# Time mixing in 11 slots with the inverse folded in, modulation products held behind the tile in front, and the normed activation made four tiles at a time

## The chip, the core and the metric

The kernel runs on one NeuronCore of a Trainium2 chip. Five engines work beside each other, each through its own list of instructions in order: TensorE (PE, with PEld for its weight loads), VectorE (DVE), ScalarE (ACT), GpSimd (POOL) and SyncE (SP), which issues nearly all transfers. An instruction that waits holds up everything behind it on its engine. The metric is the device time of one execution in microseconds (us), and less is better.

## The reference

Two layers over 256 tokens of width 2048, all in float32, one sample. Layer 0 mixes over time (RWKV-7), layer 1 is attention in chunks of 64, each followed by an MLP of width 8192 with a squared ReLU. Ahead of each part the input is normed (RMS) and modulated by a shift and a scale which come, like the gates, from the vector `c`:

```python
for layer in range(DEPTH):
    mod = c @ w_ada[layer] + b_ada[layer]
    sh1, sc1, gt1, sh2, sc2, gt2 = jnp.split(mod, 6, axis=-1)
    if layer == N_A_LAYERS:
        sh_kv, sc_kv = jnp.split(c @ w_ada_kv + b_ada_kv, 2, axis=-1)
        h_kv = modulate(rms_norm(x, g_kv), sh_kv, sc_kv)      # keys, values
    h = modulate(rms_norm(x, g_mix[layer]), sh1, sc1)
    ...                                                       # time mixing or attention
    x = x + gt1[:, None, :] * y
    h = modulate(rms_norm(x, g_mlp[layer]), sh2, sc2)
    x = x + gt2[:, None, :] * sq_relu_mlp(h, w_up[layer], w_down[layer])
return rms_norm(x, g_final)
```

Time mixing has 32 heads of 64. For each a state S runs over the tokens:

```python
sa = jnp.einsum('bhvk,bhk->bhv', S, -kk_t)
S = (S * w_t[:, :, None, :] + sa[..., None] * (kk_t * a_t)[:, :, None, :]
     + v_t[..., None] * k_t[:, :, None, :])
y = jnp.einsum('bhvk,bhk->bhv', S, r_t)
```

followed by a norm per head, a term with r, k and v, a gate, and the output projection.

## The kernel before

Activations lie with the model's 2048 channels on 16 tiles of 128 partitions, 256 tokens wide. Nearly all of the time goes to products with weights of 2048 rows. Float32 precision is made from two reduced-precision (fp32r) parts: ACT casts a weight half of 128x1024 to `wH` (L366), DVE subtracts it from the `raw` weights to give `wL` (L369), and the activation is a pair `aHL` in the same way. For each of 16 blocks of rows (kt) PE runs one 512-wide matmul with `wH` over both parts of the activation (L400) and one 256-wide matmul with `wL` (L401); a tile of 128 output channels is 16 such pairs. Transfers of weights land in a ring `raw` of six 512 KB slots, `wH` and `wL` have three slots each.

The modulation is a product of the vector `c` with 16 x 2048 columns per part; DVE makes it as running sums (`acc`, L430), one transfer of 512 KB for each, and PE adds up 128 rows at the end of 16 (L442, 128x1 matmuls). These products run between other work: a call of `ada` takes one further, and calls stand in the loops of time mixing, MLP0 and attention. In MLP0 their ring is `rawm` with six slots, in attention `rawt` with two.

Time mixing handles a pair of heads (128 channels) at a time, 16 pairs, in a pipeline four deep: while the wide matmuls project k and r for pair j, the generators `early`, `invert` and `late` run for the three pairs ahead of it. `invert` builds the inverse of a unit triangular 64x64 matrix per chunk of 64 tokens, in doubling levels of 32x32 tiles; `late` goes over the four chunks in turn and carries the state `zs`. Each round of the pipeline is cut into 16 slots; a slot runs each generator by its share of steps (up to a `yield`), then a share of the wide matmuls, and the order on PE is tied to this by `issue_after`. Small matmuls are of 64x64 or 32x32 tiles of PE's array, several side by side.

At three places, called seams here (the first tiles of MLP0, of attention and of MLP1), the next product would need x normed over all channels, which is known only when all of x is there. The first eight tiles (`SCALED`) run on x times gain without the norm, with two more columns for the shift (258-wide, L389 to L391), and are multiplied with `rstd` afterwards. `rstd` needs the sum over all channels (`m`, L494), a logarithm and an exponential on ACT (L498, L499) and some steps on DVE (L496, L501 to L504). Meanwhile `normed` makes the normed activation for the tiles from the ninth on: per channel tile a product with `rstd` on POOL (L519), two activations on ACT (L521), one subtraction on DVE (L522).

The tile framework orders each engine's instructions by its own list scheduling within the given dependencies, so an edit can also move instructions that it doesn't name.

## Time and profile before

| | us |
|---|---|
| runs shown | 2738.26 (median), 2733.71, 2740.51 |
| profiled execution | 2732.68, its span 2730.7 |
| PE busy | 2645.1 (97%) |
| DVE busy | 2041.8 (75%) |
| ACT busy | 1363.3 (50%) |
| POOL busy | 361.0 (13%) |

The span is a chain of stages: the low-rank products and the value projection to about 231 us, time mixing to 744, output projection to 806, MLP0 to 1538 (its first eight tiles to 859), attention's keys, values and scores to 1897, its output projection to 1988, MLP1 to 2717. The page gives totals of the whole span; the windows give them by stage. In the timeline a row has start, duration, engine, line, operation, output and inputs, shape and count, and in brackets the idle time ahead of it with what ended it. Matmuls overlap, so the cost of one on PE is read from start to start, not from its duration.

### The profile page before, as it was taken

How to read it: one execution, taken by the hardware profiler on the slowest of the kernel's cores; microseconds unless marked ns; L12 is line 12 of the kernel's file. 1: busy time of each engine (PE TensorE's matmuls, PEld its weight loads, DVE VectorE, ACT ScalarE, POOL GpSimd, SP SyncE). 2: the span in 40 equal slices, each digit the busy share in tenths (PEclk: the TensorE clock that was granted, in tenths of full speed). 3: DMA queues.
4: the chain of work that ended last, by engine and by line, in shares of the span. 5: the costliest groups of instructions: out<-in, count | busy, mean ns of one | idle time of the engine just before them, and what ended most of it. 6: DMA issues, size and time to landing. Idle time of an engine off the chain costs nothing.

```text
span 2730.7 us, 59448 instructions
## 1 busy us (share of the span) xinstructions
PE 2645.1 (97%) x24298; PEld 2250.2 (82%) x24298; DVE 2041.8 (75%) x2986; ACT 1363.3 (50%) x2457; POOL 361.0 (13%) x480
## 2 busy tenths in 40 slices
PE   6999999999999999999999899999999999999997
PEld 5787777777889888888888888877888888888886
DVE  5568777878799687788888788899996655566554
ACT  3346555555457543345544474465465533455443
POOL 0003434443212000000000130000120000000011
PEclk9999999999999999999999999999999999999999
DMA  9866546555688688888888778988875555555553
GB/s 349 299 243 197 172 157 191 191 170 167 214 301 286 224 284 302 316 315 315 308 307 309 249 241 310 329 307 279 283 267 194 185 190 188 187 190 186 190 188 124
DMA packets 192817, 662.70 MB, mean 243 GB/s; under 512 B 21409, under 2 KB 36129, under 8 KB 192545
## 3 DMA queue, kind: packets, MB, share of 16 engines
q1 hardware_dynamic: 190480, 656.36, 70.3%
q8 instruction: 191, 3.13, 0.5%
q10 hardware_dynamic: 2064, 2.54, 0.3%
q14 instruction: 82, 0.66, 0.1%
HBM read 656.72 MB, written 2.10 MB: 241 GB/s over the span
## 4 chain that ended last, share of the span: by engine, by line
PE 77%; DVE 7%; DMA 5%; issue 2%; ACT 2%; POOL 1%; DVEq 0%; SPq 0%; POOLq 0%; ACTq 0%
PE pj L400 41%; PE pj L401 20%; DMA rawt<-w_ada 3%; DVE wL L369 2%; PE iv L106 2%; DVE acc L430 2%; PE gr L100 1%; PE pj L391 1%; PE pj L390 1%; PE pj L389 1%; PE o L389 1%; DMA rawm<-w_ada 1%; ACT wH L366 1%; PE ms L100 1%; PE chn L279 1%
## 5 line engine op out<-in xcount | busy, mean ns | idle before, releaser
L400 PE MATMUL pj<-aHL,wH 128*128 128x512 f32 x4352 | 1574.7, 402 | 4.0 <-DVE ks L962 1.2
L369 DVE TENSOR_TENSOR wL<-raw,wH 128x1024 fp32r<-128x1024 f32 x772 | 951.5, 1234 | 421.7 <-ACT wH L366 419.1
L366 ACT CAST wH<-raw 128x1024 fp32r<-128x1024 f32 x772 | 805.9, 1046 | 878.3 <-PE pj L400 767.5
L401 PE MATMUL pj<-aHL,wL 128*128 128x256 f32 x4352 | 1226.6, 282 | 4.8 <-DVE wL L369 4.4
L400 PEld LDWEIGHTS pj<-aHL,wH 128*128 128x128 f32 x4352 | 821.2, 189 | 203.0 <-issue 11.5
L401 PEld LDWEIGHTS pj<-aHL,wL 128*128 128x128 f32 x4352 | 822.5, 189 | 12.0 <-DVE wL L369 9.5
L400 PE MATMUL pj<-hHL,wH 128*128 128x512 f32 x1024 | 359.0, 394 | 0.0
L401 PE MATMUL pj<-hHL,wL 128*128 128x256 f32 x1024 | 284.2, 278 | 0.0
L489 POOL TENSOR_TENSOR ss<-ss,sq 128x256 f32<-128x256 f32 x56 | 55.2, 986 | 1477.3 <-ACT sq L488 1477.1
L400 PEld LDWEIGHTS pj<-hHL,wH 128*128 128x128 f32 x1024 | 192.0, 188 | 44.5
L430 DVE SCALAR_TENSOR_TENSOR acc<-rawm,ct,acc 128x1024 f32<-128x1024 f32 x165 | 215.3, 1305 | 10.5 <-DMA rawm<-w_ada_kv 6.3
L401 PEld LDWEIGHTS pj<-hHL,wL 128*128 128x128 f32 x1024 | 192.3, 188 | 0.0
L430 DVE SCALAR_TENSOR_TENSOR acc<-rawt,ct,acc 128x1024 f32<-128x1024 f32 x100 | 129.7, 1297 | 21.4 <-DMA rawt<-w_ada 21.1
L430 DVE SCALAR_TENSOR_TENSOR acc<-raw,ct,acc 128x1024 f32<-128x1024 f32 x95 | 127.4, 1341 | 0.8 <-DMA raw<-w_ada 0.6
L389 PE MATMUL pj<-aHL,wH 128*128 128x258 f32 x384 | 112.4, 293 | 9.4 <-DVE ks L976 7.1
L391 PE MATMUL pj<-aHL,wL 128*128 128x258 f32 x384 | 111.4, 290 | 5.6 <-DVE wL L369 5.5
L390 PE MATMUL pj<-aHL,wH 128*128 128x258 f32 x384 | 111.7, 291 | 2.4 <-DVE aHL L513 2.4
L926 DVE SCALAR_TENSOR_TENSOR x<-pj,mod,x 128x256 f32<-128x256 f32 x128 | 61.7, 482 | 38.9 <-PE pj L401 37.2
L519 POOL TENSOR_TENSOR sq<-x,rstd 128x256 f32<-128x256 f32 x64 | 67.7, 1070 | 125.1 <-DVE aHL L522 70.7
L389 PEld LDWEIGHTS pj<-aHL,wH 128*128 128x128 f32 x384 | 75.1, 195 | 10.7 <-issue 7.3
L391 PEld LDWEIGHTS pj<-aHL,wL 128*128 128x128 f32 x384 | 75.9, 198 | 7.0 <-DVE wL L369 6.5
L390 PEld LDWEIGHTS pj<-aHL,wH 128*128 128x128 f32 x384 | 75.3, 196 | 3.0 <-DVE aHL L513 2.8
(255 smaller groups left out, 3026.6 us busy)
## 6 DMA issues: line engine op xcount, KB each, us to landing
raw<-w_up SPq DMA_DIRECT2D x256, 512.0 KB, 4.3
raw<-w_down SPq DMA_DIRECT2D x256, 512.0 KB, 3.9
rawm<-w_ada SPq DMA_DIRECT2D x111, 512.0 KB, 6.0
rawt<-w_ada SPq DMA_DIRECT2D x107, 512.0 KB, 4.7
raw<-w_ada SPq DMA_DIRECT2D x102, 512.0 KB, 4.2
rawa<-w_ada SPq DMA_DIRECT2D x64, 512.0 KB, 6.5
rawm<-w_ada_kv SPq DMA_DIRECT2D x64, 512.0 KB, 6.5
raw<-w_k SPq DMA_DIRECT2D x32, 512.0 KB, 4.0
```

Of the source, the lines that this page charges most:

```text
L100: self.b.nc.tensor.matmul(o(c)[K], lhsT(c)[K], rhs(c)[K], start=True, stop=True)
L366: nc.scalar.copy(Hf, raw)
L369: eng.tensor_tensor(out=Lf, in0=raw, in1=Hf, op=ALU.subtract)
L389: nc.tensor.matmul(ps, H[:, i, :], a(kt)[:, 0, :], start=(first and kt == 0), stop=False)
L390: nc.tensor.matmul(ps, H[:, i, :], a(kt)[:, 1, :], start=False, stop=False)
L391: ins = nc.tensor.matmul(ps, L[:, i, :], a(kt)[:, 0, :], start=False, stop=(last and kt == KT - 1))
L400: nc.tensor.matmul(ps, H[:, i, :], a(kt), start=(first and kt == 0), stop=False)
L401: ins = nc.tensor.matmul(ps[:, 0, :], L[:, i, :], a(kt)[:, 0, :], start=False, stop=(last and kt == KT - 1))
L430: nc.vector.scalar_tensor_tensor(out=acc, in0=raw, scalar=ck, in1=acc, op0=ALU.mult, op1=ALU.add)
L489: (eng or nc.gpsimd).tensor_tensor(out=self.ss, in0=self.ss, in1=sq, op=ALU.add)
L519: nc.gpsimd.tensor_tensor(out=t, in0=self.x[:, n, :], in1=rstd, op=ALU.mult)
L926: nc.vector.scalar_tensor_tensor(out=x, in0=ps[:, i, :], scalar=self.mods[(layer, 5)][:, n:n + 1], in1=x, op0=ALU.mult, op1=ALU.add)
```

## The change

1. **Time mixing.** A round has 11 slots in place of 16 (`SLOTS`); `late` has 10 steps in place of 16, `invert` 11 in place of 13, and the wide matmuls yield after each of 32 pairs of matmuls. The inverse u is not applied in each chunk (`chn<-g,uf`, then `sa`), but once for all four chunks: with `ba` holding the decayed b and the masked b-r product side by side, `ra` = -u'ba (64x128 matmuls, one 128x512 copy on ACT), and the chunk's state and output use `ra` with `g` directly. The transposed inverse is stored for it. The head of `invert` (gram matrix, four copies, `lev0` product, sum) is one step, the transposes move to the first level. The subtraction for the output's squares moves from POOL to DVE.
2. **Modulation.** `mark` notes the last DVE instruction traced before a tile's weights, and `ada` issues what it adds behind that. `ada_tick` takes two steps every second time in place of every third, so that 180 transfers in place of 160 are handled in MLP0's 120 ticks; attention has 20 fewer (its first eight key tiles call `ada` four times in place of eight, the value and query projections take 1 or 2 in turn in place of 2).
3. **Normed activation.** `normed` handles four channel tiles: one 128x1024 product with `rstd` on DVE, eight activations on ACT, one 128x4x256 subtraction on DVE; its temporary is a slot of the weights' ring `raw`. It is called after every second of the first eight tiles, and for the queries' input after keys 10 and 13 and values 0 and 4.
4. **rstd.** Its refinement has three DVE steps in place of four.

```diff
-    def parts(self, func, src, scale=1.0):
+    def parts(self, func, src, scale=1.0, eng=None):
...
-        nc.gpsimd.tensor_tensor(out=L, in0=src, in1=H, op=ALU.subtract)
+        (eng or nc.gpsimd).tensor_tensor(out=L, in0=src, in1=H, op=ALU.subtract)
...
+        pg = pp.tile([P, 4, P], F32, tag="gr", bufs=1, name="gr")
+        self.each(lambda c: pg[:, c, :], lambda c: ch(bh)[:, c, :], lambda c: kr[:, c, :])
+        da, co, u = half("da", 2), half("co", 2), half("u", 2)
+        for i, K in enumerate(QS):
+            n = H * (i % 2)
+            nc.scalar.copy(da[K], pg[K, :, n:n + H])
+        nc.gpsimd.tensor_tensor(out=u, in0=da, in1=every("lev0"), op=ALU.mult)
+        for K in QS[::2]:
+            nc.scalar.mul(co[K], pg[K, :, H:C], -1.0)
+        ba = self.ba = self.big("ba", 2)
+        nc.vector.tensor_tensor(out=u, in0=u, in1=every("eye_h"), op=ALU.add)
+        nc.vector.tensor_tensor(out=ba[:, :, C:P], in0=pg[:, :, C:P], in1=ui[:, :, C:P], op=ALU.mult)
...
-        pg = pp.tile([P, 4, P], F32, tag="gr", bufs=1, name="gr")
-        self.each(lambda c: pg[:, c, :], lambda c: ch(bh)[:, c, :], lambda c: kr[:, c, :])
-        ar = self.ar = s("ar", 2)
-        nc.vector.tensor_tensor(out=ch(ar), in0=pg[:, :, C:P], in1=ui[:, :, C:P], op=ALU.mult)
...
-        nc.gpsimd.tensor_tensor(out=u, in0=da, in1=every("lev0"), op=ALU.mult)
-        yield
-        nc.vector.tensor_tensor(out=u, in0=u, in1=every("eye_h"), op=ALU.add)
...
-        nc.scalar.copy(bk[:, 0:2], pt)
         yield
...
-        down, up = ((0, 1), (2, 3)), ((1, 0), (3, 2))
+        down, up = ((0, 1), (2, 3)), ((1, 1), (3, 3))
...
-                    nc.gpsimd.tensor_copy(uf[K, :, H * (i % 2):H * (i % 2) + H], u[K])
+                    nc.gpsimd.tensor_copy(uf[K, :, H * (i % 2):H * (i % 2) + H], tt_[K])
...
-                self.tiles(pi, xs, u, up)
-                for K in QS[::2]:
-                    nc.vector.tensor_copy(uf[K, :, H:C], pi[K])
+                self.tiles(pi, u, xs, up)
+                for K in QS[1::2]:
+                    nc.vector.tensor_copy(uf[K, :, 0:H], pi[K])
+            if l == 1:
+                pt = b.psm().rearrange("p (a c k) -> p a c k", a=2, c=4)
+                for i, t in enumerate(ts):
+                    self.each(lambda c: pt[:, i, c, :], lambda c: ch(t)[:, c, :], lambda c: cst("eye"))
+                nc.scalar.copy(ba[:, :, 0:C], pt[:, 0])
+                nc.scalar.copy(bk[:, 0], pt[:, 1])
...
+            if c == 0:
+                pr = b.psm().rearrange("p (c k) -> p c k", c=4)
+                self.each(lambda c: pr[:, c, :], lambda c: u[:, c, :], lambda c: ba[:, c, :])
+                nc.scalar.mul(ra, pr, -1.0)
...
+            if c < 3:
+                for K in heads:
+                    nc.tensor.matmul(pch[K, 1, :], bk[K, 0, c, :], bk[K, 1, c, :], start=True, stop=False)
+                for K in heads:
+                    nc.tensor.matmul(pch[K, 1, :], ra[K, c, 0:C], g[K, :], start=False, stop=True)
...
             for K in heads:
-                nc.tensor.matmul(pch[K, 1, :], u[K, c, :], g[K, :], start=True, stop=True)
-            nc.scalar.mul(sa, pch[:, 1, :], -1.0)
...
+            for K in heads:
+                nc.tensor.matmul(ch(py)[K, c, :], g[K, :], ra[K, c, C:P], start=False, stop=True)
+            if c < 3:
+                zs = zn
+            else:
+                sq = self.parts(AF.Square, py, eng=nc.vector)
...
-                for K in heads:
-                    nc.tensor.matmul(pch[K, 2, :], bk[K, 0, c, :], sa[K, :], start=False, stop=True)
...
-            for K in heads:
-                nc.tensor.matmul(ch(py)[K, c, :], sa[K, :], ch(ar)[K, c, :], start=False, stop=True)
-            yield
...
+    SLOTS = 11
     DRAIN_STEPS = (14, 14, 16)
-    ADA_SLOTS = (1, 3, 6, 9, 11, 14)
+    ADA_SLOTS = (1, 2, 4, 6, 8, 9)
...
+    def mark(self):
+        dve = self.nc.vector.engine
+        self.after = next(i for i in reversed(self.nc.cur_bb.bb.instructions) if i.engine == dve)
+
     def ada(self, n=1):
-        for _ in range(n):
-            next(self.adas, None)
+        with self.tc.issue_after(self.after) if self.after is not None else nullcontext():
+            for _ in range(n):
+                next(self.adas, None)
...
-        nc.vector.tensor_tensor(out=u, in0=y, in1=y, op=ALU.mult)
+        nc.vector.scalar_tensor_tensor(out=u, in0=y, scalar=-0.5, in1=y, op0=ALU.mult, op1=ALU.mult)
         nc.vector.tensor_tensor(out=u, in0=u, in1=v, op=ALU.mult)
-        nc.vector.tensor_scalar(out=u, in0=u, scalar1=-0.5, scalar2=1.5, op0=ALU.mult, op1=ALU.add)
-        nc.vector.tensor_tensor(out=y, in0=y, in1=u, op=ALU.mult)
+        nc.vector.scalar_tensor_tensor(out=y, in0=u, scalar=1.5, in1=y, op0=ALU.add, op1=ALU.mult)
...
-    def normed(self, hl, n, rstd, gain, sh):
+    def normed(self, hl, g, rstd, gain, sh):
         nc = self.nc
-        H, L = hl[:, n, 0, 0:T], hl[:, n, 1, 0:T]
-        t = self.np.tile([P, T], F32, tag="sq", bufs=3, name="sq")
-        nc.gpsimd.tensor_tensor(out=t, in0=self.x[:, n, :], in1=rstd, op=ALU.mult)
-        for o in (H, t):
-            nc.scalar.activation(o, t, AF.Identity, scale=gain[:, n:n + 1], bias=sh[:, n:n + 1])
-        nc.vector.tensor_tensor(out=L, in0=t, in1=H, op=ALU.subtract)
+        ns = range(4 * g, 4 * g + 4)
+        t = self.wp.tile([P, HK * P], F32, tag="raw", bufs=self.RAW_BUFS, name="raw").rearrange("p (a b) -> p a b", a=4)
+        nc.vector.tensor_tensor(out=t, in0=self.x[:, 4 * g:4 * g + 4, :],
+                                in1=rstd.unsqueeze(1).to_broadcast([P, 4, T]), op=ALU.mult)
+        for i, n in enumerate(ns):
+            for o in (hl[:, n, 0, 0:T], t[:, i, :]):
+                nc.scalar.activation(o, t[:, i, :], AF.Identity, scale=gain[:, n:n + 1], bias=sh[:, n:n + 1])
+        nc.vector.tensor_tensor(out=hl[:, 4 * g:4 * g + 4, 1, 0:T], in0=t, in1=hl[:, 4 * g:4 * g + 4, 0, 0:T],
+                                op=ALU.subtract)
...
-            stages = ((Pair.late, 16), (Pair.invert, 13), (Pair.early, Pair.EARLY), (None, 16))
+            stages = ((Pair.late, 10), (Pair.invert, 11), (Pair.early, Pair.EARLY), (None, 2 * KT))
...
-                for slot in range(16):
+                for slot in range(self.SLOTS):
...
+                self.mark()
...
                 if scaled:
-                    for i in range(f * KT // SCALED, (f + 1) * KT // SCALED):
-                        self.normed(full, i, rstd, up_gain, self.mods[up_sh])
+                    if f % 2 == 0:
+                        self.normed(full, f // 2, rstd, up_gain, self.mods[up_sh])
...
-        self.ada(2 if self.nticks % 3 == 0 else 1)
+        self.ada(2 if self.nticks % 2 == 0 else 1)
...
             between = iter(between)
+            self.mark()
...
             if j < SCALED:
+                self.mark()
...
-                for i in range(j * KT // SCALED, (j + 1) * KT // SCALED):
-                    self.normed(full, i, rstd, self.gains["g_kv"], self.mods[("kv", 0)])
-                self.ada(1)
+                if j % 2 == 0:
+                    self.normed(full, j // 2, rstd, self.gains["g_kv"], self.mods[("kv", 0)])
+                if j >= SCALED // 2:
+                    self.ada(1)
...
-                project(d["w_k_shared"][j], full, ks[:, j, :], 1 + j % 2)
-                self.normed(hq, j - SCALED, rstd, gain, self.mods[(1, 0)])
+                project(d["w_k_shared"][j], full, ks[:, j, :], 1)
+                if j in (10, 13):
+                    self.normed(hq, (j - 10) // 3, rstd, gain, self.mods[(1, 0)])
...
-            project(d["w_v_shared"][j], full, t, 2, (none, none, turn))
-            if j < SCALED:
-                self.normed(hq, KT - SCALED + j, rstd, gain, self.mods[(1, 0)])
+            project(d["w_v_shared"][j], full, t, 1 + j % 2, (none, none, none, turn))
+            if j in (0, 4):
+                self.normed(hq, 2 + j // 4, rstd, gain, self.mods[(1, 0)])
...
-                project(d["w_q"][j], hq, qs[j], 2, (none, step, score, step) if turn is none else (none, none, turn))
+                project(d["w_q"][j], hq, qs[j], 1 + j % 2, (none, step, score, step) if turn is none else (none, none, turn))
```

How the instructions move, in three places. First PE in the middle of time mixing, where `pj` is the wide product, `chn` and `py` the chunk's state and output of `late`, `iv` the inverse, `ms<-csts,s` a transpose by small matmuls; the new kernel's line numbers differ by a few. Before:

```order
L286 MATMUL chn<-g,uf_2518 64x64 x2
L289 MATMUL py<-mk,bk 64x64 x2
L100 MATMUL ms<-csts,s 64x64 x16
L400 MATMUL pj<-aHL,wH 128x512
L401 MATMUL pj<-aHL,wL 128x256
L400 MATMUL pj<-aHL,wH 128x512
L401 MATMUL pj<-aHL,wL 128x256
L296 MATMUL chn<-bk 64x64 x2
L298 MATMUL chn<-sa,bk 64x64 x2
L307 MATMUL py<-ar,sa 64x64 x2
```

After the change:

```order
L290 MATMUL chn<-bk 64x64 x2
L292 MATMUL chn<-g,ra 64x64 x2
L300 MATMUL py<-mk,bk 64x64 x2
L303 MATMUL py<-kr,zs 64x64 x2
L305 MATMUL py<-ra,g 64x64 x2
L106 MATMUL iv<-tt,al 32x32 x16
L400 MATMUL pj<-aHL,wH 128x512
L401 MATMUL pj<-aHL,wL 128x256
L400 MATMUL pj<-aHL,wH 128x512
L401 MATMUL pj<-aHL,wL 128x256
L400 MATMUL pj<-aHL,wH 128x512
L401 MATMUL pj<-aHL,wL 128x256
```

Two wide pairs stood between two groups of small matmuls, now three do, and a group holds more of a chunk's work (`chn` and all of `py` in one).

Second ACT at the first seam, where MLP0 begins. `rstd` is finished by the two activations on it; the `CAST` rows make `wH` of coming tiles. Before, the second tile's casts are `wH_12467` and `wH_12473`, the third's `wH_12545` and `wH_12551`:

```order
L366 CAST wH_12467<-raw_12465 128x1024
L512 ACTIVATE aHL_11745<-x_11709,gain_g_mlp0_11715 128x256
L488 ACTIVATE sq_12364<-x_11709 128x256
L366 CAST wH_12473<-raw_12471 128x1024
L366 CAST wH_12545<-raw_12543 128x1024
L498 ACTIVATE rstd_12441<-rv_12439 128x256
L499 ACTIVATE rstd_12441<-rstd_12441 128x256
L366 CAST wH_12551<-raw_12549 128x1024
L521 ACTIVATE aHL_12374<-sq_12455,mod_0_3_73,gain_g_mlp0_11715 128x256
```

After the change:

```order
L493 ACTIVATE sq_12299<-x_11644 128x256
L503 ACTIVATE rstd_12376<-rv_12374 128x256
L504 ACTIVATE rstd_12376<-rstd_12376 128x256
L527 ACTIVATE aHL_12309<-raw_12389,mod_0_3_73,gain_g_mlp0_11650 128x256
L909 ACTIVATE hHL_12385<-t_12323 128x256
L527 ACTIVATE raw_12389<-raw_12389,mod_0_3_73,gain_g_mlp0_11650 128x256
L910 ACTIVATE t_12323<-t_12323 128x256
L527 ACTIVATE aHL_12309<-raw_12389,mod_0_3_73,gain_g_mlp0_11650 128x256 x2
L527 ACTIVATE raw_12389<-raw_12389,mod_0_3_73,gain_g_mlp0_11650 128x256 x2
L527 ACTIVATE aHL_12309<-raw_12389,mod_0_3_73,gain_g_mlp0_11650 128x256
L366 CAST wH_12402<-raw_12400 128x1024
```

The second tile's casts and one of the third's stood ahead of `rstd`; after the change the second tile's first cast, `wH_12402`, stands behind `rstd` and behind seven activations of the first normed group (L527) and the two of the first tile's result (L909, L910). PE's next matmul after the sum `m` is the one with `wH_12402`.

Third DVE at the seam of attention, where `ks` is the key tile that is rescaled. Before:

```order
L369 TENSOR_TENSOR wL_19886<-raw_19883,wH_19885 128x1024
L430 SCALAR_TENSOR_TENSOR acc_19608<-rawt_20108,ct_68,acc_19608 128x1024
L496 TENSOR_SCALAR rv_19850<-m_19848 128x256
L369 TENSOR_TENSOR wL_19958<-raw_19955,wH_19957 128x1024
L501 TENSOR_TENSOR ru_19855<-rstd_19852 128x256
L430 SCALAR_TENSOR_TENSOR acc_19608<-rawt_20186,ct_68,acc_19608 128x1024
L502 TENSOR_TENSOR ru_19855<-ru_19855,rv_19850 128x256
L369 TENSOR_TENSOR wL_19964<-raw_19961,wH_19963 128x1024
L503 TENSOR_SCALAR ru_19855<-ru_19855 128x256
L430 SCALAR_TENSOR_TENSOR acc_19608<-rawt_20264,ct_68,acc_19608 128x1024
L504 TENSOR_TENSOR rstd_19852<-rstd_19852,ru_19855 128x256
L369 TENSOR_TENSOR wL_20036<-raw_20033,wH_20035 128x1024
```

After the change:

```order
L501 TENSOR_SCALAR rv_19843<-m_19841 128x256
L506 SCALAR_TENSOR_TENSOR ru_19848<-rstd_19845 128x256
L507 TENSOR_TENSOR ru_19848<-ru_19848,rv_19843 128x256
L508 SCALAR_TENSOR_TENSOR rstd_19845<-ru_19848,rstd_19845 128x256
L988 TENSOR_TENSOR ks_19775<-pj_19792,rstd_19845 128x256
L523 TENSOR_TENSOR raw_19856<-x_11644,rstd_19845 128x1024
L523 TENSOR_TENSOR raw_19997<-x_11644,rstd_19845 128x1024
L528 TENSOR_TENSOR aHL_19777<-raw_19856,aHL_19777 128x4x256
L369 TENSOR_TENSOR wL_19870<-raw_19867,wH_19869 128x1024
L369 TENSOR_TENSOR wL_19876<-raw_19873,wH_19875 128x1024
```

The modulation products (`acc<-rawt`) between the weights' subtractions and the steps of `rstd` are gone from this place; the `wL` rows that stood between them stand behind `rstd`, two products of the normed groups (L523) and a subtraction (L528).

More of the change, by code (lines that the diff above doesn't have):

```diff
@@ L273, in late @@
         py = pyt[:, 0, :]
+        ra = self.big("ra", 1)
         zs = None
         for c in range(4):
-            pch = pp.tile([P, 3, C], F32, tag="chn", bufs=1, name="chn")
-            g, sa = (pw.tile([P, C], F32, tag=n_, bufs=2, name=n_) for n_ in ("g", "sa"))
+            pch = pp.tile([P, 2, C], F32, tag="chn", bufs=1, name="chn")
+            g = pw.tile([P, C], F32, tag="g", bufs=2, name="g")
             for K in heads:
-                nc.tensor.matmul(pch[K, 0, :], mk[K, c, 0:C], bk[K, 2, c, :], start=True, stop=(c == 0))
+                nc.tensor.matmul(pch[K, 0, :], mk[K, c, 0:C], bk[K, 1, c, :], start=True, stop=(c == 0))
             if c:
@@ L292, in late @@
                     nc.tensor.matmul(ch(py)[K, c, :], zs[K, :], kr[K, c, C:P], start=False, stop=False)
[L293 removed]
+            for K in heads:
+                nc.tensor.matmul(ch(py)[K, c, :], g[K, :], ra[K, c, C:P], start=False, stop=True)
             if c < 3:
[L295 to L304 removed]
                 zs = zn
[L306 to L307 removed]
+            else:
+                sq = self.parts(AF.Square, py, eng=nc.vector)
             yield
         var, pg = pyt[:, 1, :], pyt[:, 1, :]
[L311 to L312 removed]
         self.head_sums(var, sq)
[L314 removed]
         rg = s("sl", 3)
@@ L486, in ss_add @@
         else:
-            sq = self.np.tile([P, T], F32, tag="sq", bufs=3, name="sq")
+            sq = self.np.tile([P, T], F32, tag="sq", bufs=2, name="sq")
             nc.scalar.activation(sq, x, AF.Square)
@@ L553, in run @@
         self.nhalf, self.pool_every = 0, 0
+        self.after = None
         self.lazy, self.fins, self.ada_ring = False, iter(()), None
@@ L954, in project @@
             between = iter(between)
+            self.mark()
             w = self.weight(wsrc)
@@ L968, in attention @@
             if j < SCALED:
+                self.mark()
                 w = self.weight(d["w_k_shared"][j])
```

49 lines of the change are left out of this document (16 added, 33 removed).

## The prediction

> **What bounds the kernel now.** I read the first page for the shares of the engines and the chain, the windows for the stages, and the timeline and waits of the stages where TensorE (PE) is not full.
>
> ```profile
> PE 2645.1 (97%) x24298; PEld 2250.2 (82%) x24298; DVE 2041.8 (75%) x2986; ACT 1363.3 (50%) x2457; POOL 361.0 (13%) x480
> GB/s 349 299 243 197 172 157 191 191 170 167 214 301 286 224 284 302 316 315 315 308 307 309 249 241 310 329 307 279 283 267 194 185 190 188 187 190 186 190 188 124
> L369 DVE TENSOR_TENSOR wL<-raw,wH 128x1024 fp32r<-128x1024 f32 x772 | 951.5, 1234 | 421.7 <-ACT wH L366 419.1
> L366 ACT CAST wH<-raw 128x1024 fp32r<-128x1024 f32 x772 | 805.9, 1046 | 878.3 <-PE pj L400 767.5
> ```
>
> PE is busy 97%; the second row is the rate of transfers in 40 slices. By stage (start:end, length, then PE, PEld, DVE, ACT, POOL busy, clock, DMA share, GB/s):
>
> ```profile
> 231.00:744.00 513.00, 498.45 (x9422) 391.30 (x9421) 410.29 (x752) 264.68 (x736) 205.37 (x268) 0.99 0.56 179
> 806.00:859.00 53.00, 50.20 (x448) 48.57 (x447) 47.42 (x71) 36.72 (x65) 15.17 (x17) 0.97 0.79 268
> 859.00:1538.00 679.00, 679.00 (x4418) 591.95 (x4417) 547.56 (x647) 323.69 (x443) 14.15 (x14) 1.00 0.84 295
> 1538.00:1597.00 59.00, 50.79 (x390) 49.76 (x389) 46.31 (x59) 37.05 (x66) 21.40 (x27) 0.91 0.78 257
> 1597.00:1755.00 158.00, 152.48 (x1049) 131.18 (x1048) 130.26 (x141) 81.53 (x126) 14.43 (x13) 1.00 0.87 302
> 1755.00:1897.00 142.00, 137.99 (x975) 105.29 (x974) 135.50 (x292) 83.38 (x222) 7.20 (x56) 1.00 0.88 295
> 1897.00:1988.00 91.00, 87.92 (x609) 74.52 (x608) 82.29 (x99) 43.83 (x63) 12.30 (x14) 1.00 0.82 278
> 1988.00:2043.00 55.00, 48.59 (x383) 47.64 (x382) 50.77 (x71) 37.04 (x64) 18.15 (x16) 0.94 0.80 274
> 2043.00:2717.00 674.00, 672.43 (x3908) 587.02 (x3907) 382.74 (x482) 322.03 (x441) 15.82 (x14) 1.00 0.55 184
> ```
>
> These are time mixing, the first eight tiles of MLP0, its rest, the first eight of attention, keys and values, scores, the output projection, the first eight of MLP1, its rest. The rests of the MLPs have no idle PE: nothing can be won there. Mixing has 14.6 us of idle PE, the rows of eight tiles 2.8, 8.2 and 6.4, keys and values, scores and projection 5.5, 4.0 and 3.1. What can be won lies in these idle times, and in what keeps PE busy without need; that needs the order of single matmuls:
>
> ```profile
> 400.57 0.28 PE L298 MATMUL chn<-sa,bk 64*64 64x64 f32 x4
> 400.69 0.28 PE L307 MATMUL py<-ar,sa 64*64 64x64 f32 x4
> 400.90 0.50 PE L400 MATMUL pj<-aHL,wH 128*128 128x512 f32 x1
> 401.24 0.28 PE L401 MATMUL pj<-aHL,wL 128*128 128x256 f32 x1
> 401.36 0.40 PE L400 MATMUL pj<-aHL,wH 128*128 128x512 f32 x1
> 401.59 0.28 PE L401 MATMUL pj<-aHL,wL 128*128 128x256 f32 x1
> 401.80 0.31 PE L442 MATMUL ms<-csts,acc 128*32 128x1 f32 x16
> 402.03 0.33 PE L279 MATMUL chn<-bk,mk 64*64 64x64 f32 x4
> 402.20 0.28 PE L282 MATMUL chn<-zs,kr 64*64 64x64 f32 x4
> 402.80 1.09 PE L100 MATMUL gr<-kr,kh 64*64 64x128 f32 x16
> 403.82 0.50 PE L400 MATMUL pj<-aHL,wH 128*128 128x512 f32 x1
> ```
>
> From start to start a wide pair (L400, then L401) costs 0.23 + 0.12 = 0.35 us, and four small ones 0.12. But the first L400 behind small tiles takes 0.34 (+0.11); the last small group takes 0.21 (+0.09); the L401 before small tiles 0.21 (+0.09); the first small group 0.17 (+0.05). One return from small tiles to wide ones and back so costs 0.34 us on PE, and the page calls it busy.
>
> **Time mixing.** In the order of PE's instructions I counted the returns from small to wide: 272 before, 230 after, since a pair is cut into 11 slots and not 16. 42 x 0.34 = 14.3 us less. The number of matmuls stays, but 128 of 64x64 become 64x128: at 1.02/16 = 0.064 (the last two rows) against 0.12/4 = 0.030 us that is 128 x 0.034 = 4.4 more. Issue: **-10**. The waits of PE in this stage (us in total, times, longest):
>
> ```profile
> PE py L123 <- POOL sL L118: 7.6, 4, 2.2
> PE iv L106 <- DVE tt L238: 3.8, 5, 2.0
> ```
>
> The first is the subtraction of `parts` for the output's squares on POOL; it goes to DVE, in this place alone: **-7** (bounds 0 and -7.6). The second is the inverse, whose 13 steps become 11 with some 40% more wide work between two of them: **-3** (0 to -3.8). New are waits where yields are gone: the gram matrix, four copies on ACT, POOL's `lev0` product, DVE's sum and transpose stand in one step, eight links of 0.3 to 0.5 us (the nearest rows are L503 and L521 below), 2.4 to 4 us against a slot of 513/19/11 = 2.5 (19 rounds of 11); `ra` is waited for too. I take 0.25 us a pair, **+4** (0 to 16, at 1 us a pair): nearer to nothing, since PE idles less than 1 us a pair now with chains of the same kind. Together mixing is **-16**, with bounds of -25 and +6.
>
> **The three seams.** Behind each output projection or MLP, 8 tiles run on unnormed input and are rescaled once `rstd` is there. What stands there now:
>
> ```profile
> 813.87 0.39 PE L390 MATMUL pj<-aHL,wH 128*128 128x258 f32 x1 [1.79 <-DVE aHL L513]
> 1550.12 1.28 DVE L430 SCALAR_TENSOR_TENSOR acc<-rawt,ct,acc 128x1024 f32<-128x1024 f32 x1 [1.86 <-DMA rawt<-w_ada]
> 1559.49 0.55 PE L389 MATMUL pj<-aHL,wH 128*128 128x258 f32 x1 [7.11 <-DVE ks L976]
> 2015.86 0.58 PE L391 MATMUL pj<-aHL,wL 128*128 128x258 f32 x1 [3.97 <-DVE wL L369]
> ```
>
> DVE's modulation products (L430) stand in front of `wL` there and wait for their transfers; `mark` puts them behind, which takes these waits away. But the order of the change has something new: at each seam ScalarE's cast of the second tile, which stood ahead of `rstd`, stands behind it and behind seven or eight activations of the first `normed` group of four. PE's next matmul needs that cast. Its price, from the same operations at the kernel's clean end:
>
> ```profile
> 2717.56 0.70 PE L494 MATMUL m<-ss,csts 128*128 128x256 f32 x2 [2.13 <-DVE ss L489]
> 2720.57 0.29 DVE L503 TENSOR_SCALAR ru<-ru 128x256 f32<-128x256 f32 x1
> 2721.36 1.22 DVE L588 TENSOR_TENSOR x<-x,rstd 128x1024 f32<-128x1024 f32 x1
> 2016.80 1.09 ACT L521 ACTIVATE aHL<-sq,mod,gain_g_mlp 128x256 fp32r<-128x256 f32 x2
> 2017.80 1.08 ACT L521 ACTIVATE sq<-sq,mod,gain_g_mlp 128x256 f32<-128x256 f32 x2
> ```
>
> From the sum's matmul to `rstd` 2721.36 - 2717.56 = 3.8, less one step (L503, 0.33) = 3.5. The product with the f = 0 tile 0.35, the 128x1024 product 1.22. Nine activations at 0.50 (2.00 us would be four, by the last two rows) 4.5. Cast 1.05, `wL` 1.23. **11.9 us** in which PE stands still, at each of three seams. Behind such a stop the clock is low:
>
> ```profile
> 811.00:818.00 7.00, 4.81 (x23) 4.23 (x22) 5.86 (x11) 3.63 (x6) 0.00 (x0) 0.76 0.92 331
> 2010.00:2020.00 10.00, 4.65 (x23) 4.44 (x24) 9.82 (x13) 8.37 (x15) 4.87 (x5) 0.66 0.71 246
> ```
>
> 0.76 over 7 us is half clock for 3.4 us (1.7 lost); 0.66 over 10 is half for 6.8 (3.4 lost). I take 2.5: 14.4 a seam, 43 in all. [...]
>
> What the seams lose now follows from the undisturbed step:
>
> ```profile
> 818.08 0.29 PE L389 MATMUL pj<-aHL,wH 128*128 128x258 f32 x1
> 818.20 0.28 PE L390 MATMUL pj<-aHL,wH 128*128 128x258 f32 x1
> ```
>
> Eight tiles are 8 x 48 = 384 steps of 0.12, 46 us. The rows of 53, 59 and 55 us are 167 in all, less 3 x 46.5 (some small matmuls beside) leaves 27. 43 - 27 = **+16**, the largest term against the change. Bounds: 0 if the casts were hidden after all, +24 if each stop costs 5 us of clock.
>
> **Attention.** In the value and query projections each tile of 16 pairs (16 x 0.35 = 5.6 us) asked for two weight halves and two modulation halves of 0.524 MB: 2.1 MB, 374 GB/s, over the 349 that any slice of the page has. Now it asks for 1.5 halves of modulation: 1.84 MB, 328 GB/s; keys 281. The idle PE there, 5.5 us, is mostly behind late `wL` and transposes that wait for their tile, which now come one step later: **-4** (0 to -5.5). Scores and output projection idle 7.1; fewer modulation products on a DVE that is 95% busy in the one and 90% in the other: **-4** (0 to -7).
>
> **MLP0.** 20 modulation halves come here from attention, 160 to 180 in 120 ticks. DVE gets 20 x 1.28 = 26 us on 548 of 679: covered. The transfers are nearer to a limit: 20 x 0.524 MB / 679 us = 15 GB/s more than 295; in the steady part
>
> ```profile
> 985.00:1160.00 175.00, 175.00 (x1123) 152.53 (x1122) 139.15 (x146) 68.25 (x70) 0.00 (x0) 1.00 0.89 311
> ```
>
> 311 becomes about 327, at a share of 0.94. I take **+1** (0 to 35, below). The normed work moves from POOL to DVE, 16 x (1.22 + 1.23) against 64 x 0.42, 12 us more, under 8 tiles at each seam: covered by 5.6 us tiles on which DVE has some 3.5 us. The temp in the weights' ring takes one of six slots for a few us: nothing. One step less in the first and the last `rstd`: 2 x 0.33, **-0.7**.
>
> Sum: -16 + 16 - 4 - 4 + 1 - 0.7 = **-7.7**. The profiled execution took 2732.7 us, 2730.7 of it the span, so 2725; it lies 5.6 us under the median of the runs, 2738.3. Against that median, which the new median is held to: 2730.6, in round numbers **2730**.
>
> **Rivals.**
> - The seams cost no more than now (something else in front of PE, or stops that the profile before already has in full). For it: 27 us are lost there now. Against: the order is fixed, and PE has nothing else to run. Then -16 - 4 - 4 + 1 - 0.7 = -24: 2715.
> - The chains of the longer steps set the pace in mixing: 1 us a pair in place of 0.25, +12. For it: the head's 4 us against 3.4. Against: PE idles only 14.6 us in 16 pairs now. Then +4: 2743, no change.
> - Transfers fall short in MLP0, which makes the change **slower**. Place: 679 us with PE at 100%; mechanism: at 327 GB/s wanted, late weights stop PE in each tile. It decides from a rate of 318 downwards: 679 x (327/318 - 1) = 19 in place of 1, a sum of +10; at 311 it is 35 and +26: 2764. For it: no row of that stage shows more than 311. Against: 331 at 811:818, and 349 in the first slice.
>
> **Chances.** Forecast 0.40, seams 0.20, chains 0.20, transfers 0.20. A measurement of this kernel tells about 0.3% (8.2 us) from no change; the forecast itself lies at this border, between -1 and -15. Faster: 0.23 of the forecast, 0.19, 0.01, 0.01 = 0.44; same: 0.16 + 0.01 + 0.16 + 0.03 = 0.36; slower 0.20. The likeliest case alone spans 2723 to 2738. The range reaches from 2706, the seam rival with a full gain in mixing, to 2748, a third into the transfer rival.
>
> **What would show it.** Mixing about 16 us shorter and the wait of `py` for `sL` gone from POOL: the first terms. One stop of 11 to 13 us at each seam, named after `wH` or `wL`, with a clock under 0.7 in the 20 us around it: the seams. PE at 100% and 320 to 330 GB/s in MLP0: the transfers are held. Wrong I would be most likely about the seams: if PE's longest wait there is under 5 us, the sum loses its only large loss.

## The result: 2710.8 us, a ratio of 0.9905

The change takes 2710.8 us (median; 2709.7 to 2713.4) against 2739.2 for the kernel before in the same place (2733.7 to 2740.5): ratio 0.9905, 95% interval 0.9891 to 0.9918. It is faster by 28 us. The forecast was 2730, faster by 8, with the time inside its range of 2706 to 2748.

Stage by stage the gain is not where the sum had it. The rows of the windows of the changed kernel, in the same order and columns as those of before (without the output projection of the mixing and the rest of MLP1):

```profile
231.00:716.00 485.00, 479.12 (x9414) 386.41 (x9413) 410.84 (x768) 263.36 (x704) 174.33 (x252) 1.00 0.59 188
779.00:839.00 60.00, 49.97 (x388) 49.18 (x387) 39.72 (x54) 38.33 (x66) 0.00 (x0) 0.89 0.46 150
839.00:1520.00 681.00, 681.00 (x4548) 593.59 (x4547) 588.89 (x682) 324.70 (x441) 11.11 (x14) 1.00 0.90 317
1520.00:1580.00 60.00, 49.52 (x387) 48.77 (x386) 40.17 (x44) 36.90 (x66) 0.92 (x8) 0.89 0.66 224
1580.00:1737.00 157.00, 153.05 (x987) 132.14 (x987) 117.19 (x121) 82.41 (x128) 0.00 (x0) 0.99 0.85 289
1737.00:1877.00 140.00, 139.42 (x993) 107.70 (x992) 131.36 (x286) 83.03 (x222) 7.07 (x56) 1.00 0.80 263
1877.00:1965.00 88.00, 83.23 (x587) 71.15 (x586) 81.95 (x98) 42.12 (x61) 14.52 (x14) 1.00 0.77 261
1965.00:2024.00 59.00, 48.97 (x397) 48.26 (x388) 39.35 (x55) 38.42 (x66) 0.00 (x0) 0.91 0.70 240
```

Mixing is shorter by 28 us at a clock of 1.00, the three seams (second, fourth and last row) are 59 to 60 us long with 10 us of idle PE each, and MLP0 holds 317 GB/s with PE busy throughout. What PE waited for, in the whole execution:

```profile
PE pj L389 <- ACT wH L366: 29.6, 4, 9.6
...
PE iv L106 <- DVE tt L230: 1.0, 2, 0.8
...
PE py L123 <- DVE sL L118: 0.3, 1, 0.3
```

29.6 us for the casts at the seams, and next to nothing of the mixing's old waits (7.6 and 3.8). One seam in the timeline, MLP0's:

```profile
785.36 0.60 PE L499 MATMUL m<-ss,csts 128*128 128x256 f32 x2
...
789.07 1.22 DVE L523 TENSOR_TENSOR raw<-x,rstd 128x1024 f32<-128x1024 f32 x1
...
790.38 0.60 ACT L527 ACTIVATE aHL<-raw,mod,gain_g_mlp 128x256 fp32r<-128x256 f32 x1 [3.06 <-DVE raw L523]
...
794.45 1.03 ACT L366 CAST wH<-raw 128x1024 fp32r<-128x1024 f32 x1
...
795.51 1.23 DVE L369 TENSOR_TENSOR wL<-raw,wH 128x1024 fp32r<-128x1024 f32 x1 [1.83 <-ACT wH L366]
795.53 0.58 PE L389 MATMUL pj<-aHL,wH 128*128 128x258 f32 x1 [9.57 <-ACT wH L366]
...
796.79 0.58 PE L391 MATMUL pj<-aHL,wL 128*128 128x258 f32 x1 [0.46 <-DVE wL L369]
```

The product with `rstd`, nine activations in 4.1 us (seven of the normed group, two of the first tile's result), the cast, `wL`: PE stands 9.57 + 0.46 = 10 us, and its next matmuls take 0.58 us at a granted clock of 0.50, where the same ones take 0.28 at 1.00.

For what follows, the stage lengths in us, each read from the start of the stage's first matmul to that of the next stage. "First 8" is the seam's eight tiles. E1 to E8 are explained below.

| | before | change | E1 mixing | E2 modulation | E3 normed | E4 casts first | E8 normed as before |
|---|---|---|---|---|---|---|---|
| mixing | 537.7 | 510.4 | 510.8 | 538.4 | 539.2 | 511.9 | 511.2 |
| MLP0, first 8 | 53.6 | 59.8 | 51.6 | 49.1 | 65.4 | 47.6 | 49.2 |
| MLP0, rest | 679.3 | 680.8 | 678.9 | 680.7 | 679.9 | 680.8 | 680.7 |
| attention, first 8 | 58.5 | 60.1 | 59.8 | 53.2 | 65.0 | 47.2 | 52.5 |
| keys and values | 158.3 | 156.9 | 159.6 | 155.8 | 157.3 | 156.0 | 155.5 |
| scores | 141.9 | 139.5 | 141.7 | 139.5 | 143.5 | 139.4 | 139.9 |
| projection | 90.2 | 88.3 | 89.9 | 88.0 | 89.9 | 88.2 | 89.2 |
| MLP1, first 8 | 55.7 | 59.4 | 55.2 | 49.2 | 66.2 | 47.7 | 49.2 |
| time, median | 2739.2 | 2710.8 | 2708.8 | 2715.3 | 2764.7 | 2675.5 | 2688.5 |

### The profile page after: what moved, and what is told of

Read it like the earlier page. It is cut to its first block, busy times and chain, and to the rows that moved or that the text cites. A ratio compares the mean times of both kernels' runs of the same rounds, so it can differ in the third digit from the quotient of the medians.

```text
span 2711.6 us, 59299 instructions
## 1 busy us (share of the span) xinstructions
PE 2623.6 (97%) x24298; PEld 2248.0 (83%) x24298; DVE 2043.4 (75%) x2965; ACT 1364.2 (50%) x2425; POOL 260.8 (10%) x400
## 4 chain that ended last, share of the span: by engine, by line
PE 82%; DVE 5%; DMA 3%; ACT 2%; issue 1%; POOL 1%; DVEq 0%; SPq 0%; POOLq 0%; ACTq 0%
PE pj L400 43%; PE pj L401 22%; DMA rawt<-w_ada 3%; PE iv L106 2%; PE pj L391 2%; PE pj L389 2%; PE pj L390 2%; PE ms L100 1%; DVE acc L430 1%; DVE wL L369 1%; PE gr L100 1%; PE o L389 1%; PE py L320 1%; PE chn L278 0%; ACT wH L366 0%
## 5 line engine op out<-in xcount | busy, mean ns | idle before, releaser
L369 DVE TENSOR_TENSOR wL<-raw,wH 128x1024 fp32r<-128x1024 f32 x772 | 941.5, 1221 | 377.5 <-ACT wH L366 371.8
L430 DVE SCALAR_TENSOR_TENSOR acc<-rawm,ct,acc 128x1024 f32<-128x1024 f32 x184 | 235.5, 1280 | 0.9
L389 PE MATMUL pj<-aHL,wH 128*128 128x258 f32 x384 | 112.6, 293 | 29.6 <-ACT wH L366 29.6
L430 DVE SCALAR_TENSOR_TENSOR acc<-rawt,ct,acc 128x1024 f32<-128x1024 f32 x81 | 104.0, 1284 | 33.9 <-DMA rawt<-w_ada 33.6
L430 DVE SCALAR_TENSOR_TENSOR acc<-raw,ct,acc 128x1024 f32<-128x1024 f32 x95 | 123.7, 1302 | 1.0 <-DMA raw<-w_ada 0.7
L639 PE MATMUL m<-rawa,crep 128*32 128x128 f32 x1024 | 42.2, 293 | 14.1 <-DMA rawa<-w_ada 13.5
```

What stands on the lines that cost most here:

```text
L369: eng.tensor_tensor(out=Lf, in0=raw, in1=Hf, op=ALU.subtract)
L389: nc.tensor.matmul(ps, H[:, i, :], a(kt)[:, 0, :], start=(first and kt == 0), stop=False)
L430: nc.vector.scalar_tensor_tensor(out=acc, in0=raw, scalar=ck, in1=acc, op0=ALU.mult, op1=ALU.add)
```

## The experiments

**E1 to E3: each part alone.** The change has three parts that the diff separates; each was put alone into the kernel before.

```diff
 E1  stages = ((Pair.late, 10), (Pair.invert, 11), (Pair.early, Pair.EARLY), (None, 2 * KT))   # SLOTS = 11, ba, ra
 E2  self.mark() ... issue_after(self.after) ... self.ada(2 if self.nticks % 2 == 0 else 1)    # and attention's numbers
 E3  self.normed(full, f // 2, rstd, up_gain, self.mods[up_sh])                                # groups of four, rstd in three steps
```

Mixing:

> The kernel before with the time mixing part alone: 11 slots, inverse folded into ra, subtraction of the squares on DVE. Theory: the whole gain of the change lies here, some 27 us by the span from the first wide matmul of mixing to its last output (537.7 to about 510), so the time is 2712 (ratio 0.990), and the seams keep what they lose now (53.6, 58.5, 55.7 us). Rival, modulation: mixing gives only the 16 us of the forecast, 2723 (0.994), and the rest came from the products held behind the tile in front.

Measured: 2708.8, ratio 0.9902 (0.9882 to 0.9921). The mixing part by itself is worth as much as the whole change, and nearly all of it lies in the mixing stage (26.9 of the 28.4 us between the two profiled executions). The theory of 27 us holds, the forecast's 16 does not.

Modulation:

> The kernel before with the modulation part alone: mark and the order behind it, a tick of two every second time, fewer products in attention, transposes of the values one step later. Theory: the seam of attention loses its 7.1 us wait and that of MLP0 1.8, scores 3, keys and values 1, MLP0 takes 1 more: -8 to -12, 2729 (0.9965). Rival, transfers: MLP0 at 328 GB/s stops PE, its 679 us become 690 or more, and the sum is 0 or above. Rival, modulation as the main part: -15 or more.

Measured: 2715.3, ratio 0.9928 (0.9908 to 0.9948), twice what I expected. MLP0 did not suffer (680.7), so the rival of the transfers falls. Of the 23 us between the profiled executions 16 lie at the seams, -4.5, -5.3 and -6.5, and 7 in keys and values, scores and projection. The third seam is one that the theory had not counted: MLP1's seam has modulation products in front of `wL` too. DVE there, before:

```profile
2011.72 1.75 DVE L430 SCALAR_TENSOR_TENSOR acc<-rawm,ct,acc 128x1024 f32<-128x1024 f32 x1
...
2014.06 1.74 DVE L369 TENSOR_TENSOR wL<-raw,wH 128x1024 fp32r<-128x1024 f32 x1
```

`wL` started at 2014.06, behind a modulation product that it has nothing to do with and two small subtractions, and PE waited 3.97 us for it. In E2 no L430 is left in that stretch, and PE's longest wait at that seam is 1.2 us in place of 4.0.

Normed:

> The kernel before with the normed activation four tiles at a time on DVE (temporary in the raw ring) and the three-step rstd alone. Theory: the casts of the second tile stand behind rstd and four to seven activations, so each seam has one stop of 8 to 12 us; the three seams are 167 us now and become 180 to 190, the time 2752 to 2758 (1.005 to 1.007). Rival: the stops were those of the modulation products, the grouping costs nothing, 2739 (1.000).

Measured: 2764.7, ratio 1.0106 (1.0086 to 1.0125), slower by 28 us. The mechanism is as expected, its size is not: the seams add up to 197 us, 29 more than before.

```profile
PE pj L389 <- ACT wH L366: 45.6, 4, 15.4
```

The longest stop, at attention's seam, is 15.4 us, since here DVE still has modulation products between the steps of `rstd` (two of 1.28 us between `rv` at 1561.80 and `ks` at 1566.73), and the cast then waits another 0.9 us for its weights. In the change, where `mark` has taken them away, it is 9.6. So the parts do not add up: alone -28, -22 and +28 make -22, together they made -28.

**E4: the casts first.** If the stops come from the place of the casts in ACT's list, calling the normed groups later should remove them, with the same work in the kernel:

```diff
-                    if f % 2 == 0:
-                        self.normed(full, f // 2, rstd, up_gain, self.mods[up_sh])
+                    if f in (2, 3, 5, 6):
+                        self.normed(full, (2, 3, 5, 6).index(f), rstd, up_gain, self.mods[up_sh])
```

and the same for the keys.

> The change, with the four normed groups of each seam called after tiles 2, 3, 5 and 6 and not after 0, 2, 4 and 6, which puts the casts of tiles 1 and 2 ahead of the group's activations on ACT. Theory: PE has 11 us of tiles to run while rstd and the first group are made, the three stops of 9.6 us and their low clock go, and the seams fall from 59.8, 60.1, 59.4 to about 50 each: 2683 (0.9795). Rival: the stop only moves behind tile 2 or in front of tile 8, where the groups are late, and the time stays within 5 us of the change's 2711.

Measured: 2675.5, ratio 0.9780 (0.9759 to 0.9801): 35 us under the change, and the fastest version here. The seams in E4, MLP0, attention, MLP1:

```profile
781.00:829.00 48.00, 47.30 (x391) 46.96 (x390) 38.83 (x54) 38.10 (x67) 0.00 (x0) 1.00 0.57 185
1509.00:1557.00 48.00, 47.71 (x392) 47.24 (x391) 40.45 (x46) 37.10 (x67) 0.92 (x8) 1.00 0.68 234
1940.00:1988.00 48.00, 47.30 (x429) 46.99 (x419) 39.04 (x55) 37.47 (x66) 0.00 (x0) 1.00 0.71 251
```

PE is full and its clock is never lowered; 8 tiles of 48 steps of 0.12 us are 46 us. PE runs the second and third tile while `rstd` and the first group are made. That settles the cause of the stops: the order on ACT, not the amount of work on ACT or DVE.

**E5 and E6: slots or folding.** The mixing part has two ideas. E5 has 11 slots with the inverse applied per chunk as before, E6 is the change with 16 slots:

```diff
 E5  stages = ((Pair.late, 16), (Pair.invert, 13), (Pair.early, Pair.EARLY), (None, 2 * KT))   # SLOTS = 11
 E6  SLOTS = 16; ADA_SLOTS = (1, 3, 6, 9, 11, 14)                                                # rest as in the change
```

> The kernel before with 11 slots in a round but the inverse applied in each chunk as before (late 16 steps, invert 13). By the returns from small to wide matmuls (256 in place of 272) and the changes of tile kind PE's issue falls by 7 us. Theory that the slots lift the stalls: longer slots cover the chains, the waits of iv for tt at the pipeline's start (3.4 us) and of py for sL (7.6) go, and with them the low clock behind them (some 7 us), so mixing falls by 20 or more, 2717. Theory that the folding lifts them: 7 only, 2730.

> The whole change but with 16 slots and the old places of the modulation steps. Returns 262 in place of 230, PE's issue 8 us over the change. If the shorter chain of late and invert (folding) lifts the stalls, mixing is 518 in place of 510 and the time 2719; if the long slots do it, the stalls and the low clock come back and mixing is 530 or more, 2731.

Measured: E5 2720.7, 0.9941 (0.9925 to 0.9957), mixing 528.1; E6 2719.6, 0.9936 (0.9921 to 0.9951), mixing 520.4. Neither theory of E5 holds as written: 528 lies between. The two waits that it names do go with the slots alone, `iv` for `tt` from 3.8 to 0.2 us and `py` for `sL` from 7.6 to 0.4, with the subtraction still on POOL:

```profile
PE py L123 <- POOL sL L118: 0.4, 1, 0.4
```

But others came in their place: PE is still idle for 10.6 us of mixing (14.6 before), and one stretch of low clock is left (0.73 in the window of 490 to 500 us). E6 is not the folding alone, since it also has the subtraction on DVE: its 17 us belong to the two together. With E7, below, the three pieces can be told apart as they were added: the slots 10 (537.7 to 528.1), the folding on top of them 8 (528.1 to 520.3, E7), the subtraction on top of both 10 (520.3 to 510.4). The slots on top of the other two are worth 10 as well (520.4 to 510.4), where the 32 fewer returns from small to wide matmuls were priced at 8. The folding without either of the others was not tried.

**E7: the subtraction on POOL.** One line of the change undone:

```diff
-                sq = self.parts(AF.Square, py, eng=nc.vector)
+                sq = self.parts(AF.Square, py)
```

> The whole change with the subtraction for the output's squares back on POOL (16 instructions). Theory: it is what kept py waiting (7.6 us in 4 waits, with 1.7 us of low clock behind one of them), so mixing grows by 6 to 9 us, 2718. Rival: in longer slots POOL's subtraction is ready in time as well, and the time stays at 2711.

Measured: 2719.0, 0.9930 (0.9915 to 0.9945), 8 us over the change; mixing 520.3.

```profile
PE py L123 <- POOL sL L118: 7.1, 11, 1.7
```

The wait is back in total (7.1 us) but in eleven places, and with it a window of low clock in mixing, which E6 and the change don't have:

```profile
280.00:290.00 10.00, 10.00 (x158) 8.10 (x159) 7.28 (x14) 4.75 (x15) 4.04 (x8) 0.83 0.58 191
```

So in the change that term of the prediction, -7, was right in mechanism and size, and longer slots do not cover it there. In E5, without the folding, they do; what in the folding makes the subtraction on POOL too late was not tried by itself.

**E8: the change without its normed part.**

> The change without its normed part: mixing and modulation alone, normed per channel tile with its product on POOL, rstd in four steps. If the parts add up, 2737 - 28 - 22 = 2687, and the seams are near 50 us each as with the modulation part alone. Against the change with the casts first (2675.5) it tells what the grouping itself is worth: nothing if this comes to 2675, some 10 us if it comes to 2687. Rival: without the L430 waits the stops of the change come from something else, and the seams stay near 60.

Measured: 2688.5, 0.9824 (0.9805 to 0.9842), where the parts' sum says 2687. So in the change the grouping, with `rstd`'s shorter form, costs 22 us (2710.8 - 2688.5); with the casts first it brings 13 (2675.5 - 2688.5). The seams of E8 are 49.2, 52.5 and 49.2 us, E4's 47.6, 47.2 and 47.7, which is 8 of these 13. One more us lies in the other stages, and the rest is not in the traces: E8's profiled execution is the fastest of its runs (2686.6), E4's the slowest (2677.2), so their spans differ by 9.4 only.

**E9 and E10: the order or the numbers.** The modulation part split: `mark` alone, and the numbers alone (20 products from attention to MLP0, transposes later).

```diff
 E9   self.mark()                                   # and issue_after in ada
 E10  self.ada(2 if self.nticks % 2 == 0 else 1)    # and attention's numbers, no mark
```

> The kernel before with mark and the order behind it alone; the numbers of modulation products per tick and per stage stay. Theory: the 22 us of the modulation part are the L430 rows in front of wL at the three seams, so the seams come to 49, 53 and 49 us as with the whole part, 16 to 17 us less, and the time is 2720 (0.994). Rival: without fewer transfers in attention the products behind the tile still wait for them, the attention seam stays at 58, and the gain is 10 at most.

> The kernel before with the numbers alone (20 products moved from attention to MLP0, transposes of the values one step later), without mark. Theory: keys and values 2, scores 2, projection 2 less, MLP0 1 more: 5 us in all, 2732 (0.998), seams as before except that of attention, which has half of its products left (up to 5 less). Rival, transfers: they are the larger part, 12 or more.

Measured: E9 2724.7, 0.9956 (0.9941 to 0.9971); E10 2736.3, 1.0002 (0.9990 to 1.0014). The order is worth 12 us, the numbers by themselves nothing, both together 22 (the intervals of E2 and E9 just overlap). At attention's seam each alone leaves a long wait, with `mark` alone (first row) for the key tile, with the numbers alone (second row) for a modulation product:

```profile
PE pj L389 <- DVE ks L987: 5.3, 1, 5.3
PE m L442 <- DVE acc L430: 5.6, 1, 5.6
```

The seam is 55.8 us in E9, 61.3 in E10 and 53.2 in E2. The theory for E9 was right for the two MLP seams (49.1 and 49.2). Attention's lies between the theory's 53 and the rival's 58: there a key tile's result (`ks`, L987) comes late by 5.3 us with all eight products still called; that they wait for their transfers in a ring of two slots is my reading, and was not tried by itself.

**E11: nine slots on E4.**

> The change with the casts first (2675.5) and 9 slots in place of 11. Returns from small to wide matmuls 198 in place of 230, PE's issue 6 us less by the prices of the kernel before. Theory: if issue still sets the pace, mixing is 505 in place of 511 and the time 2669. Rival: two steps of a chain now stand in some slots, and the waits inside a slot take back 6 us or more: 2675 to 2685.

Measured: 2699.2, 0.9864 (0.9846 to 0.9883), 24 us slower than E4. Mixing stays at 511 where issue alone would give 505. The output projection behind it has a new stop:

```profile
PE o L389 <- ACT wH L366: 12.2, 2, 11.0
```

It is 78 us long in place of 63, and the projection after attention 102 in place of 88. Neither can be put down to the nine slots, since the edit changed more than it names: `ADA_SLOTS` stayed at (1, 2, 4, 6, 8, 9), and a round of nine slots, 0 to 8, never comes to slot 9. So mixing handles 88 modulation products in place of E4's 102, and what is missing comes later, 9 of them in the output projection (none in E4) and 27 in place of 19 in the projection after attention. At the new stop DVE makes six in a row, in slots of the weights' ring, while the cast waits for its weights:

```profile
719.27 7.88 DVE L430 SCALAR_TENSOR_TENSOR acc<-raw,ct,acc 128x1024 f32<-128x1024 f32 x6
...
726.83 0.41 ACT L366 CAST wH<-raw 128x256 fp32r<-128x256 f32 x1 [8.56 <-DMA raw<-w_o]
```

What nine slots are worth with all six modulation steps in a round was not tried; mixing itself did not get shorter, even with 14 products less.

## Why the prediction was right in sign, and where its sum failed

By the two profiled executions (spans 2730.7 and 2711.6) the change gained 19.1 us, against a sum of -7.7:

| term | predicted | measured |
|---|---|---|
| mixing | -16 | -27.3 |
| three seams | +16 | +11.5 |
| keys and values | -4 | -1.4 |
| scores and projection | -4 | -4.3 |
| MLP0 | +1 | +1.5 |
| output projection of mixing | none | +1.2 |
| `rstd` | -0.7 | not to be told apart |

*Mixing* is the step that failed, by one term that was missing: it gained 27.3 us against 16, more than the bound of 25 that I gave it. PE's idle time in the stage fell from 14.6 to 5.9 us, by 8.7, where my terms for the waits had -7 - 3 + 4 = -6: the wait for `sL` went from 7.6 to 0.3, that for `tt` from 3.8 to 1.0, and in place of the new wait of 4 there are about 3 (1.2 for `xs`, 1.1 for another `sL`, 0.8 for `zs`). Missing was the clock. In the profile of before mixing runs at a low clock in two places:

```profile
250.00:262.00 12.00, 11.24 (x142) 8.28 (x142) 7.98 (x12) 2.96 (x11) 6.65 (x8) 0.57 0.51 169
350.00:360.00 10.00, 7.82 (x73) 6.18 (x74) 6.12 (x9) 4.42 (x14) 5.20 (x8) 0.83 0.49 158
```

0.43 of 12 us and 0.17 of 10 are 6.9 us lost, an estimate by the granted clock. The same windows of the change:

```profile
250.00:262.00 12.00, 10.88 (x180) 8.23 (x182) 10.26 (x18) 5.92 (x15) 6.18 (x9) 1.00 0.76 229
350.00:360.00 10.00, 9.39 (x238) 7.53 (x236) 10.00 (x19) 6.48 (x18) 4.38 (x6) 1.00 0.69 218
```

8.7 + 6.9 leave 11.7 of the 27.3 for PE's issue, a remainder and not a measurement, where the prediction had 10. I priced a stop at the seams with its restart, and gave the low clock in mixing, which stands in the same profile, no term.

*The profile and the median.* The other 9 us, from 19 by profile to 28 by medians, lie in the same place. E10 has the order of PE's instructions in mixing of the kernel before, and the same waits (`py` for `sL` 7.6 us in 4, `tt` 4.2), and takes 546.1 us for it:

```profile
290.00:300.00 10.00, 10.00 (x80) 7.21 (x80) 4.70 (x11) 3.42 (x12) 0.74 (x2) 0.67 0.29 95
440.00:450.00 10.00, 8.73 (x182) 6.40 (x176) 6.56 (x11) 3.24 (x11) 3.12 (x4) 0.83 0.50 148
610.00:620.00 10.00, 10.00 (x95) 7.68 (x93) 4.81 (x10) 4.62 (x15) 1.16 (x3) 0.62 0.25 75
```

where the profile of before shows a full clock:

```profile
290.00:300.00 10.00, 9.55 (x120) 7.50 (x121) 6.04 (x13) 5.42 (x17) 3.04 (x7) 1.00 0.52 167
440.00:450.00 10.00, 9.32 (x166) 7.02 (x168) 8.43 (x12) 4.57 (x13) 5.02 (x5) 1.00 0.58 183
610.00:620.00 10.00, 10.00 (x208) 7.75 (x207) 9.45 (x15) 6.78 (x17) 3.63 (x5) 1.00 0.71 224
```

3.3 + 1.7 + 3.8 = 8.8 us lost there alone, and 8.4 is the difference in length. Three more profiles have the same order of PE in mixing, E2, E3 and E9. Over the whole stage the five (before, E2, E3, E9, E10) lose 6.9, 8.5, 10.2, 11.9 and 15.4 us by the granted clock and take 537.7, 538.4, 539.2, 542.3 and 546.1; without the loss all are between 529 and 531. So how often the clock falls in the old mixing differs from one execution to the next; it would explain why the runs of before lie between 2730 and 2747 in the last comparison, and why its one profile, with few of these falls, lies under the median. The versions with the folded inverse and 11 slots (change, E1, E4, E8) show no such window in mixing, and the change's runs lie within 4 us. Among the 41 runs of before beside E1 to E11 the fastest (2724.3) has a mean granted clock of 0.994, the slowest (2747.3) one of 0.988, which is 16 of the 23 us between them. That low clock makes up the whole of the 9 us is argued from these figures, since for a single run only the mean clock is known and not the stage. Setting the sum against one profiled execution, 5.6 us under the median, I carried this difference into the forecast without its cause.

*The seams* were right: the stop after the sum `m`, its place, the cast at its end, and the low clock. The chain of 11.9 us from the start of `m` to the end of `wL` took 11.4 in MLP0: `m` starts at 785.36, and the matmul that waits for `wL` at 796.79. That PE stands still for 10.0 of them and not for all is since it runs `m` itself (0.6 us), and two matmuls on the new cast while `wL` is made. Lost in all, against the 46.5 us of work that the prediction took: 13.3, 13.6 and 12.9, where it had 14.4 each; together 40 us, where it had 43. E4 shows the cause, E8 the price. The rival that the seams cost no more than now (0.20) is refuted: they cost 11.5 more. But the bound of 0 "if the casts were hidden after all" was wrong: with no new stops most of the 27 us that the seams lost would go as well, because `mark` takes their waits away. E4 is that case, and its seams are 25 us shorter than before.

*The transfers* (0.20, the slower case): 317 GB/s as a mean over MLP0 with PE at 100%, and 323 in the steady part, where 327 were asked for:

```profile
966.00:1141.00 175.00, 175.00 (x1181) 152.41 (x1181) 141.46 (x149) 67.79 (x70) 0.00 (x0) 1.00 0.92 323
```

*The chains* (0.20): PE idles 5.9 us in all of mixing's 485; refuted. *Keys and values* gained 1.4 of the 4: the wait for the transposes fell (2.4 to 1.0), late `wL` did not (1.2), the wait for `ks` grew from 1.2 to 1.7, and 3.4 us at a granted clock of 0.50 behind it, at 1635 us, cost 1.7.

What the prediction did not see is that the order held by `mark` is worth 12 us alone and 22 with the numbers (E2, E9). I set the waits in front of `wL` against the new stops as one number; they are in the 27 us, so the sum was right about them, but the split was not told.

*Luck.* That the time lies in the range is in part luck. Its lower end, 2706, came from the rival on the seams, which is refuted; the measured 2710.8 is near it for another reason, the low clock of the mixing, in the change's favour twice: 6.9 us in the profile of before, and some 9 between that profile and the median. The likeliest case alone, 2723 to 2738, was missed.

*Smaller slips of the working.* The bound of -25 for mixing is not the sum of its terms' bounds, -10 - 7.6 - 3.8 = -21.4. That no row of MLP0 shows more than 311 GB/s overlooks the slices of the page, with 316, 315 and 315 in that stage: the rival's limit of 318 was nearer to what had been seen than was said. The chains' rival sets 4 us against a slot of 3.4, which the working has as 2.5. The old subtractions of the normed activation take 0.50 us on average (L522, 64 in 31.5 us) and not 0.42, so DVE gets 8 us more and not 12.

## What to carry to other kernels

Work that waits for a late result must not be put in an engine's list ahead of work that is ready and that the critical engine needs next: here nine activations ahead of a cast cost 22 us, and the same work called two tiles later brought 13. Price a stall with its restart wherever TensorE works in short pieces, also where no single wait is long (here 6.9 us lost by the granted clock in mixing before, with no wait over 2.2 us), and compare the clock of more than one execution before a sum is made against one. When parts of a change meet at one place (here the three seams), time them alone and together: -28, -22 and +28 came to -28, not -22. And when the number of slots of a loop changes, change everything that names a slot by its number with it: E11 lost a modulation step in every round to a slot that was no longer there.
